# A hybrid decoder layer: six PSUM banks as one tile, loads of the opening moved, memory tokens transposed raw, sample columns kept on chip

## The chip, the cores and the metric

The kernel runs on one core of one Trainium2 chip, in one launch. Its five engines work side by side, each on its own list of instructions: TensorE (PE) multiplies matrices into PSUM, VectorE (DVE) and ScalarE (ACT) do the elementwise work and read PSUM out, GpSimd (POOL) does a little elementwise work in SBUF, and SyncE (SP) issues nearly all DMAs, in order. The metric is the time of the launch on the device in microseconds; the median of several runs is compared, and one further execution is recorded by the hardware profiler.

## The reference

One layer of a decoder for 1024 prompt tokens and 8 sample tokens that share the weights, D = 1024, all in float32:

```
xn = rmsnorm(x)
sc_b, sc_c, sc_x, z, xbc, dt, q, gates = split(xn @ w_in)       # one matrix for all
y_a = (sc_b * conv3(sc_c * sc_x)) @ w_sc_out
xs, B, C = split(silu(conv4(xbc) + bias));  dt = softplus(dt + dt_bias)
y_b = group_rmsnorm((ssd(xs, dt, -exp(a_log), B, C) + d * xs) * silu(z)) @ w_ssm_out
k, v = rmsnorm(mem) @ w_mem_k, rmsnorm(mem) @ w_mem_v           # 256 memory tokens
y_c = softmax(q @ k.T / 16) @ v @ w_attn_o                      # 4 heads x 256
x += (sig(g_a) * y_a + sig(g_b) * y_b + sig(g_c) * y_c) @ w_merge_o
x += (silu(rmsnorm(x) @ w_gate) * (rmsnorm(x) @ w_up)) @ w_down   # 2816 wide
y  = rmsnorm(x)
```

The sample tokens go through the same layer, with cached keys, values, convolution histories and states of their own. The outputs are y for both groups, the memory's keys and values, and the new histories and states.

## The kernel before

**Tiling.** Channels lie on the 128 partitions, tokens along the free axis: 1032 columns, of which the first 1024 are the prompt's and the last 8 the samples'. An operand is kept as two fp32r tiles, a high part (a rounding copy by ScalarE) and a low part (the difference, by VectorE), and a product takes three matmuls: high by high, high by low, low by high. Every weight block and every activation passes through such a split (weights, L162 to L169; split_act, L175 to L179; split_to).

**Two kinds of large product.** gemm (L200) makes one block of 128 output channels for all 1032 columns, in three PSUM banks; L220 is its matmul. strassen (L311) makes two blocks of output channels at once by seven half-size products instead of eight. Each product is st_prod (L260): 24 matmuls, L266, into a pair of banks (516 columns), and each is followed by a read-out, by ScalarE's copy (L321) or VectorE's add or subtract (L319, L380, L395, L398, L408). The weight sums that it needs are made by VectorE (L361, L362, L299, L300) and split (L253 high, L254 low).

**PSUM.** There are eight banks. psm holds two single banks for everything small, taken in turn (sm_ps). The other six are held by one pool at a time. While gemms run, that is pmm: two slots of three banks, taken in turn (mm_ps, L67). While Strassen calls run, it is a pool of three tiles of two banks, with tags m0, m1 and m2 (st_ps). The change from one kind to the other closes one pool and opens the next, four times in all: in front of Z2, behind G18, in front of the feed-forward network and behind d16. A call of strassen takes its first pair (pa), its second (pb) and, where all seven products are needed, its third (pc); calls take the tags forward and backward in turn, apart from the first two calls.

**Order.** The program is written in an order that a list scheduler then makes into one list for each engine: an instruction that is ready early may be moved forward. Three means hold it: in_turn keeps the weight loads and splits in order, issue_after holds an instruction behind another without a wait, and small steps in a queue, pend, are called one by one from within the products by tick(). All loads and most stores are issued by SyncE in list order, and a load whose buffer is not free, or whose source in DRAM is not written yet, holds everything behind it. Staging tiles come from ev, a ring of five; raw weights, high parts and low parts from three rings of three.

**The opening (L461 to L643).** x is loaded in nine token blocks. In three groups of columns (g3 = 0, 1, 2) TensorE transposes x (L549), ScalarE copies the raw transposes out (L530) and SyncE stores them to xT_d (L531); VectorE scales the transposes by the norm (L533), and the result is split (L534, L535). As the groups come, the products of dt (L566, into ps_dt) and of the first B block (L576, into ps_B0) are made. Behind the loop come four blocks of convolution histories: load (L618), eight transposes (L621), copy (L622). Then dt's bias is loaded (L641) and ps_dt is read out with it (L643); two small constants are loaded in the middle of the work of dt (L681, L723). The block C0 follows: its weights, the convolution of B0 (uB, L837; first tap L754 on ScalarE for the prompt's columns, L755 and L758 on VectorE for the samples'), the first half of the Strassen forms (make_raw, L1221 and following, then the splits L416 and L417), C0's gemm, the other half of the forms, z0 (L856) and z1.

**The memory tokens (L1260 to L1325).** Between the products of Z2 and Z4, steps from pend load the 256 tokens, square them (L1274), take the root, scale the tokens by it (L1277), and transpose them in four batches of four (L1284), each batch in one bank. For each of a batch's four transposes ScalarE writes the high part (L1288) and VectorE the low part (L1289), both scaled by the norm's weight and both from PSUM. The K/V products follow in sixteen steps (kv_block), read out by a copy.

**The attention output.** The sample tokens' attention result is transposed into o_s, columns of the tile tri (L1609), and stored to the last eight columns of at_d in DRAM (L1610). Three output products follow one another (out_part); the last takes at_d as operand. out_load (L1400) loads a block of 1032 columns, and the splits L178 and L179 make it an operand. At the end of the kernel down (L1985) adds products of three hidden blocks at a time (pd, read by L2000), behind the last Strassen call d16.

Of the kernel before, what the change touches and what calls it, by code (L numbers as in the profile page):

```python
# [9 lines left out]
F32 = mybir.dt.float32  # L10
# [37 lines left out]
def tile_kernel(ctx: ExitStack, tc, a, o):  # L48
# [14 lines left out]
    psm = ctx.enter_context(tc.tile_pool(name="psm", bufs=2, space=PSUM))  # L63
    mm_stack = ExitStack()
    pmm = [mm_stack.enter_context(tc.tile_pool(name="pmm", bufs=2, space=PSUM))]

    def mm_ps(name):  # L67
        return pmm[0].tile([P, NCH, 512], F32, tag="mm", name=name)

# [163 lines left out]
    HS = [slice(0, HT), slice(HT, TT)]  # L233
    pst = [None]
    freed = [None]
# [21 lines left out]
    def st_ps(tag, name):  # L257
        return pst[0].tile([P, 2, 512], F32, tag=tag, name=name)

# [51 lines left out]
    def strassen(  # L311
# [22 lines left out]
        elif ready is None and early is None:  # L334
            raw1, raw2 = st_raw(src1, f"{nm}r1"), st_raw(src2, f"{nm}r2")
        if count[0] == 0:
            tags = ("m2", "m1", "m0")
        elif count[0] == 1:
            tags = ("m1", "m2", "m0")
        else:  # L340
            tags = ("m0", "m1", "m2") if count[0] % 2 == 0 else ("m2", "m1", "m0")
        count[0] += 1
# [99 lines left out]
    os_d = dram("os_d", [NS, D])  # L442

    tail_sc = cp.tile([P, 1, 10, 8], F32, tag="tail_sc", name="tail_sc")
    tail_xc = cp.tile([P, 3, 11, 8], F32, tag="tail_xc", name="tail_xc")
# [14 lines left out]
    xw = [act_tile(("ah", "al")[k % 2], f"xw{k}", F32) for k in range(KD)]  # L460
    ps_dt, ps_b0 = mm_ps("ps_dt"), mm_ps("ps_B0")  # L461

    with tc.tile_pool(name="p0", bufs=1) as p0:
# [59 lines left out]
        for i in range(3, NCK):  # L523
            load_x(i)
        SY.dma_start(xs_sb, a["x_sample"][:, 0, :])

        def to_xn(k, c, ps, n, name):
# [60 lines left out]
        for g3 in range(3):  # L588
            c, n_all = span(g3)
            for k in range(KD):  # L590
# [12 lines left out]
        while products:  # L603
            products.popleft()()
        for k in range(KD):
            b_product(2, k)
# [3 lines left out]

    for src, dst, nr, nt in (
        (a["state_ssm_conv"][0].rearrange("b j c -> (b j) c"), h_xc, 24, 24),
        (a["state_conv"][0].rearrange("b j c -> (b j) c"), h_sc, 16, 8),
    ):
        per = 8
        for q0 in range(0, nt, per):
            t = ev_tile(f"hist{nr}_{q0}", (nr, per * P))
            SY.dma_start(t, src[:, q0 * P : (q0 + per) * P])  # L618
            ps = sm_ps(f"ps_h{nr}_{q0}")
            for i in range(per):  # L620
                PE.transpose(ps[:, i * nr : (i + 1) * nr], t[:, i * P : (i + 1) * P], ident[:nr, :nr])  # L621
            V.tensor_copy(dst[:, q0 : q0 + per, :].rearrange("p a b -> p (a b)"), ps[:, : per * nr])  # L622
    SY.dma_start(o["s_conv"][0, :, 0, :], a["state_conv"][0, :, 1, :])
# [14 lines left out]
    pd_ = dt_stack.enter_context(tc.tile_pool(name="pdt", bufs=1))  # L638
    bias = pd_.tile([2 * HEADS, 1], F32, tag="bias", name="bias")
    V.memset(bias, 0.0)  # L640
    SY.dma_start(bias[:HEADS], a["ssm_dt_bias"].rearrange("l h -> h l"))  # L641
    dtr = ev_tile("dtr", (2 * HEADS, TT))
    V.tensor_scalar(dtr[:, :TT], flat(ps_dt)[: 2 * HEADS], bias, None, op0=ALU.add)  # L643
    W = 9 * HEADS
# [9 lines left out]
    def dt_softplus():  # L654
# [14 lines left out]
        V.scalar_tensor_tensor(u, x0, -1.0, x0, op0=ALU.mult, op1=ALU.min)  # L669
        S.activation(u, u, AF.Exp)  # L670
        V.tensor_scalar(z, u, 2.0, None, op0=ALU.add)
# [7 lines left out]
        V.scalar_tensor_tensor(dt_flat, q, 2.0, mx, op0=ALU.mult, op1=ALU.add)  # L679
        abc = pd_.tile([P, HEADS], F32, tag="abc", name="abc")  # L680
        SY.dma_start(abc, a["ssm_a_log"][0:1, :].to_broadcast([P, HEADS]))  # L681
        S.activation(abc, abc, AF.Exp)
        V.scalar_tensor_tensor(
# [34 lines left out]
    def dt_sample():  # L718

        esm = pd_.tile([NS, HEADS], F32, tag="esm", name="esm")  # L720
        S.activation(esm, da[:NS, 8, :], AF.Exp)
        exp2 = pd_.tile([16, 2], F32, tag="exp2", name="exp2")
        SY.dma_start(exp2, a["ssm_d"].rearrange("l (t two) -> (l t) two", two=2))  # L723
        ex = pd_.tile([16, 2, 64], F32, tag="ex", name="ex")
# [17 lines left out]
    def proj(col, name):  # L742
        return gemm(weights(wblock(w_in, col), "w" + name), xn, "ps_" + name)

    def conv(acc, u, hist, key, ct, nt, taps, bias):

# [3 lines left out]
        if bias is None:  # L750
            S.activation(acc[:, :T], u[:, 0:T], AF.Copy, scale=w[0])
            V.tensor_scalar(ap_s, hv[:, :, 0], w[0], None, op0=ALU.mult)
        else:
            S.activation(acc[:, :T], u[:, 0:T], AF.Identity, scale=w[0], bias=bias)  # L754
            V.tensor_scalar(ap_s, hv[:, :, 0], w[0], bias, op0=ALU.mult, op1=ALU.add)  # L755
# [470 lines left out]

    def make_forms(k0):
        mk = fx_tile if k0 == 0 else act_pair
        raws = [make_raw(kt) for kt in (k0, k0 + 1)]
        for i, f in enumerate(("T1", "nT2", "T4")):  # L1230
# [39 lines left out]

    def mem_rms():
        for m in range(2):
            junk = memT[m][0].rearrange("p k c -> p (k c)")
            S.activation(junk, mem_sb[m], AF.Square, accum_out=mst[:, m : m + 1])  # L1274
        rsqrt(pm, mrs, mst, D, [P, 2], "m")
        for m in range(2):
            V.tensor_scalar(mem_sb[m], mem_sb[m], mrs[:, m : m + 1], None, op0=ALU.mult)  # L1277

    def mem_t(m, half):
        hi, lo = memT[m]  # L1280
        ps = sm_ps(f"ps_mt{m}{half}")
        for k4 in range(4):
            k = half * 4 + k4
            PE.transpose(ps[:, k4 * P : (k4 + 1) * P], mem_sb[m][:, k * P : (k + 1) * P], ident)  # L1284
        for k4 in range(4):
            k = half * 4 + k4
            pk = ps[:, k4 * P : (k4 + 1) * P]
            S.activation(hi[:, k, :], pk, AF.Copy, scale=par("mem", k))  # L1288
            V.scalar_tensor_tensor(  # L1289
                lo[:, k, :], pk, par("mem", k), f32(hi)[:, k, :], op0=ALU.mult, op1=ALU.subtract  # L1290
            )

    pss_kv = []

    def kv_block(j, q):
# [24 lines left out]
    pend.extend([None, mem_rms, None])  # L1320
    pend.extend(lambda m=m, half=half: mem_t(m, half) for m in range(2) for half in range(2))
    pend.extend(lambda j=j, q=q: kv_block(j, q) for j in range(8) for q in range(2))
    pace[0] = 5
# [6 lines left out]

    mm_stack.close()
    mm_stack = ExitStack()
    st_stack = ExitStack()
    pst[0] = st_stack.enter_context(tc.tile_pool(name="pst1", bufs=1, space=PSUM))
    for i in (2, 4, 6, 8, 10, 12):
# [42 lines left out]
    gate_pair(18, plain)  # L1378
    st_stack.close()
    pa_stack.close()  # L1380
    ch_stack.close()
    pmm[0] = mm_stack.enter_context(tc.tile_pool(name="pmm1", bufs=2, space=PSUM))

# [14 lines left out]
    def out_load(src, k):  # L1398
        t = ev_tile(f"in0{k}")
        SY.dma_start(t[:, :TT], src[k])  # L1400
        ahead.append(t)
# [98 lines left out]
    if True:  # L1500
# [3 lines left out]
        vl = at.tile([P, 2, D], F32R, tag="vl", bufs=1, name="vl")  # L1504
        o_s = tri[:, :64].rearrange("p (t b) -> p t b", t=8)
        sc_s = tri[:, 64:].rearrange("p (m b h) -> p m b h", m=2, b=NS)
# [96 lines left out]
        def s_back():  # L1603
# [5 lines left out]
            V.tensor_copy(o_s.rearrange("p t b -> p (t b)"), ps[:, :64])  # L1609
            SY.dma_start(at_d[:, :, T:TT].rearrange("t p b -> p t b"), o_s)  # L1610

# [209 lines left out]
    aux_stack.close()  # L1821
    mm_stack.close()

# [3 lines left out]
    st_stack = ExitStack()  # L1827
    pst[0] = st_stack.enter_context(tc.tile_pool(name="pst", bufs=1, space=PSUM))
    pfx = st_stack.enter_context(tc.tile_pool(name="fx", bufs=2))
# [135 lines left out]
    st_stack.close()  # L1965
    pmm[0] = ctx.enter_context(tc.tile_pool(name="pmm2", bufs=2, space=PSUM))
    fin = ctx.enter_context(tc.tile_pool(name="fin", bufs=1))
# [131 lines left out]
```

## Time and profile before

| | |
|---|---|
| median of 3 runs | 2475.04 us (2474.16 to 2475.89) |
| the profiled execution | 2474.8 us, span 2472.7 us |
| granted TensorE clock, mean | 0.994 |
| TensorE busy | 2428.5 us (98%) |
| VectorE, ScalarE, GpSimd busy | 1584.3, 1067.1, 114.8 us |
| opening up to the first C0 matmul | 58.73 us |
| C0, z0, z1 up to the first Strassen matmul | 58.73 to 98.74 us |
| DMA | 404.42 MB, mean 164 GB/s |

A page of the profile gives for each engine the time in which it executes, and for each group of instructions how long its engine stood idle before it and which instruction ended that (the releaser). In a timeline a row is: start in us, duration in us, engine, line, operation, output <- input, shape, count, and in brackets the idle time before and the releaser. A row with a count gives several instructions in one. The table of stretches gives, for each, its length, the busy time of each engine with the number of its instructions, the granted TensorE clock (1.00 is full speed), the share of the DMA engines and GB/s.

### The profile page before, as it was taken

What the parts mean: (1) busy time and instruction counts of PE and PEld (TensorE: products, weight loads), DVE (VectorE), ACT (ScalarE), POOL (GpSimd) and SP (SyncE); (2) the same over time, 40 slices, a digit from 0 to 9 for tenths busy, and PEclk for the clock granted to TensorE, in tenths of its full rate; (3) what the DMA queues carried; (4) which work ended last, traced back from release to release, by engine and by line L of the source; (5) the groups of instructions that cost most, each with busy time, mean ns of one, the idle gap of its engine ahead of it and who ended that gap; (6) DMA issues with size and microseconds to landing.
All of it is one profiled execution on the core that took longest, in us unless ns stands there. A gap on an engine that the chain in (4) does not pass through costs nothing.

```text
span 2472.7 us, 45688 instructions
## 1 busy us (share of the span) xinstructions
PE 2428.5 (98%) x18946; PEld 2310.5 (93%) x18946; DVE 1584.3 (64%) x2601; ACT 1067.1 (43%) x1712; POOL 114.8 (5%) x163
## 2 busy tenths in 40 slices
PE   8999999999999999999999999999999999999998
PEld 6899999999999999888888888899999999999998
DVE  6844586777677774666767562454787555476755
ACT  6654455354545535556545441223453333342322
POOL 0100000000000000121120000000000000000000
PEclk8999999999999999999999999999999999999999
DMA  6344434344344456667878677874454323264421
GB/s 195 121 139 154 132 102 153 112 130 131 108 137 137 129 154 210 194 207 254 265 219 286 205 265 238 266 241 153 141 174 134 108 86 112 74 231 132 156 85 69
DMA packets 359662, 404.42 MB, mean 164 GB/s; under 512 B 17446, under 2 KB 286870, under 8 KB 359447
## 3 DMA queue, kind: packets, MB, share of 16 engines
q1 hardware_dynamic: 339006, 343.79, 44.6%
q10 hardware_dynamic: 20449, 57.71, 6.0%
q8 instruction: 149, 2.44, 0.4%
q14 instruction: 58, 0.48, 0.1%
HBM read 286.35 MB, written 115.32 MB: 162 GB/s over the span
## 4 chain that ended last, share of the span: by engine, by line
PE 86%; DMA 5%; DVE 5%; ACT 2%; issue 1%; SPq 0%; ACTq 0%; POOL 0%; DVEq 0%
PE po L220 12%; PE ps_q L220 4%; PE pm L1800 3%; PE ps_g L220 2%; PE pd L220 1%; PE py L1041 1%; PE pss L1054 1%; PE po L1033 1%; PE Z2m L266 1%; PE Z4m L266 1%; PE X8m L266 1%; PE d12m L266 1%; PE C2m L266 1%; PE C4m L266 1%; PE G18m L266 1%
## 5 line engine op out<-in xcount | busy, mean ns | idle before, releaser
L986 ACT ACTIVATE r<-r,acum 128x128 f32<-128x128 f32 x256 | 79.2, 392 | 5.1 <-DMA r<-ac_d 4.7
L757 DVE SCALAR_TENSOR_TENSOR ax<-u,prm,ax 128x1024 f32<-128x1024 f32 x44 | 56.3, 1279 | 0.0
L927 ACT ACTIVATE st<-st,es 128x128 f32<-128x128 f32 x128 | 41.5, 392 | 26.4 <-DMA st<-in_state_ssm_dram 23.9
L1018 POOL TENSOR_TENSOR xdd<-xdt,decst 128x512 f32<-128x512 f32 x32 | 37.1, 1160 | 292.2 <-DVE xdt L1014 292.2
L1447 DVE TENSOR_TENSOR yr<-po,yr 128x1032 f32<-128x1032 f32 x8 | 9.8, 1230 | 55.1 <-PE po L220 45.2
L1037 DVE TENSOR_TENSOR y<-po,ea 128x512 f32<-128x512 f32 x28 | 19.3, 690 | 38.9 <-PE po L1033 38.9
L1012 DVE TENSOR_TENSOR r<-r,cbm 128x1024 f32<-128x1024 f32 x32 | 39.2, 1224 | 2.5
L929 DVE SCALAR_TENSOR_TENSOR st<-sr,dts,st 128x128 f32<-128x128 f32 x128 | 40.3, 345 | 0.4
L1011 ACT COPY bT<-bp 128x128 f32<-128x128 f32 x32 | 8.5, 265 | 64.3 <-DVE cbm L1009 64.2
L2034 ACT ACTIVATE fj<-psy 128x512 f32<-128x512 f32 (+1 forms) x18 | 10.7, 596 | 59.1 <-PE psy L2032 59.0
L933 DVE SCALAR_TENSOR_TENSOR sr<-st,sr 128x128 f32<-128x128 f32 x128 | 35.2, 285 | 1.1
L1054 PE MATMUL pss<-xdd,bT 128*128 128x512 f32 x64 | 33.4, 604 | 2.3 <-ACT bT L1011 2.3
L1041 PE MATMUL py<-r,xdt 128*64 128x128 f32 x512 | 35.0, 279 | 0.0
L987 ACT ACTIVATE r<-r 128x1024 f32<-128x1024 f32 x32 | 33.9, 1058 | 0.7
L1014 DVE TENSOR_TENSOR xdt<-xp,dtT 128x512 f32<-128x512 f32 x32 | 21.9, 684 | 18.7 <-PE xp L1007 18.5
L1807 DVE TENSOR_TENSOR x<-pm,xT 128x516 f32<-128x516 f32 x16 | 11.1, 695 | 35.1 <-PE pm L1800 35.1
L1067 POOL TENSOR_TENSOR s<-s,cdec 128x512 f32<-128x512 f32 x28 | 32.1, 1145 | 4.5 <-DVE s L1060 3.9
L1041 PEld LDWEIGHTS py<-r,xdt 128*64 128x64 f32 x512 | 27.3, 136 | 4.2 <-issue 0.5
L1033 PE MATMUL po<-bc,s 128*128 128x128 f32 x224 | 29.6, 275 | 0.0
L760 DVE SCALAR_TENSOR_TENSOR ax<-u,prm,ax 128x1032 f32<-128x1032 f32 x22 | 28.3, 1286 | 0.0
L1178 DVE SCALAR_TENSOR_TENSOR x<-x,prm,sqa 128x1032 f32<-128x1032 f32 x16 | 19.7, 1288 | 13.3 <-ACT sqa L1174 13.3
L1033 PEld LDWEIGHTS po<-bc,s 128*128 128x128 f32 x224 | 27.7, 191 | 0.5
(9066 smaller groups left out, 9044.0 us busy)
## 6 DMA issues: line engine op xcount, KB each, us to landing
r<-ac_d SPq DMA_DIRECT2D x32, 512.0 KB
gt<-gt_d SPq DMA_DIRECT2D x24, 516.0 KB
xs_d<-ax ACTq DMA_DIRECT2D x22, 516.0 KB
gt_d<-G ACTq DMA_DIRECT2D x20, 516.0 KB
x<-xs_d SPq DMA_DIRECT2D x16, 516.0 KB
zs<-zs_d SPq DMA_DIRECT2D x16, 516.0 KB
yb_d<-x SPq DMA_DIRECT2D x16, 516.0 KB
in<-yb_d SPq DMA_DIRECT2D x16, 516.0 KB
```

The source lines that it names most:

```text
L220: PE.matmul(out[:, c : c + n], wt[:, ks], x[:, c : c + n], start=(k == 0 and i == 0), stop=(k == nk - 1 and i == 2),)
L266: PE.matmul(hv(ps)[:, c : c + n], wt[:, ks], x[:, c : c + n], start=(start and kt == 0 and i == 0), stop=(kt == 3 and i == 2), skip_group_ ...
L757: V.scalar_tensor_tensor(acc[:, :T], u[:, j : j + T], w[j], acc[:, :T], op0=ALU.mult, op1=ALU.add)
L927: S.activation(st[:, i], st[:, i], AF.Copy, scale=es[:, g * 4 + i, b : b + 1])
L929: V.scalar_tensor_tensor(st[:, i], rb, dts[:, g * 4 + i, b : b + 1], st[:, i], op0=ALU.mult, op1=ALU.add)
L986: S.activation(r[:, j, :], r[:, j, :], AF.Relu, scale=-1.0, bias=acum[:, c, h : h + 1])
L1012: V.tensor_tensor(r, r, bc(cbm.unsqueeze(1), [P, HPG, P]), op=ALU.mult)
L1018: G.tensor_tensor(b3(xdd, HPG), b3(xdt, HPG), bc(decst[:, c, hs].unsqueeze(2), [P, HPG, 64]), op=ALU.mult)
L1033: PE.matmul(po[:, t * P : (t + 1) * P], state["s"][:, t * P : (t + 1) * P], bcg[1][:, cs], start=True, stop=True,)
L1041: PE.matmul(py[hp : hp + 64, (h // 2) * P : (h // 2 + 1) * P], xdt[:, h * 64 : (h + 1) * 64], r[:, (h % 2) * 4 + h // 2, :], start=True, s ...
L1054: PE.matmul(pss, bT, xdd, start=True, stop=True)
L1800: PE.matmul(hv(ps)[:, c : c + n], wt[:, ks], x[:, half * HT + c : half * HT + c + n], start=(k == 0 and i == 0), stop=(k == KD - 1 and i = ...
```

## The change

Four parts, in one:

- **Six banks as one tile.** pmm and the Strassen pools go; one tile, six, of six banks lives through the whole kernel. mm_ps gives its lower or its upper three banks in turn (side); st_ps gives the pair of banks 0-1, 2-3 or 4-5 by the tag. The tags now go forward and backward in turn from the first call on, and each call sets the side that the next gemm will take. In the opening ps_B0 has the lower side and ps_dt the upper one, and C0 takes the upper.
- **The opening.** The bias and the two constants are loaded right behind x, into a pool that stays. The raw weights of C0 are loaded at the beginning of group 1; those of z0 and z1 and the four history blocks at the beginning of group 2. ps_dt is read out as soon as the dt products are done, ahead of the last group of B0's products, and C0's weights are split right behind that. The forms, C0 and z0 are held behind the last history copy (past) and the first tap of B0's convolution (tap). Of the four make_raw only two stand ahead of that mark. The Exp of the decay is held behind the Exp of dt.
- **The memory tokens** are transposed as loaded. VectorE multiplies a whole batch by the norm's weight out of PSUM, back into the tile of the tokens; ScalarE copies the high part and VectorE subtracts, both from SBUF. The root comes behind the transposes, and K and V are scaled by it when they are read out.
- **The sample columns.** The store to at_d's last eight columns goes; out_load takes 1024 columns from at_d and copies the other eight from o_s, with GpSimd.

```diff
+    six = pbig.tile([P, 2 * NCH, 512], F32, tag="six", name="six")
+    side = [0]
     def mm_ps(name):
-        return pmm[0].tile([P, NCH, 512], F32, tag="mm", name=name)
+        i = side[0]
+        side[0] = 1 - i
+        return six[:, NCH * i : NCH * (i + 1)]
...
     def st_ps(tag, name):
-        return pst[0].tile([P, 2, 512], F32, tag=tag, name=name)
+        i = int(tag[1:])
+        return six[:, 2 * i : 2 * i + 2]
...
+        tags = ("m0", "m1", "m2") if count[0] % 2 == 0 else ("m2", "m1", "m0")
+        side[0] = 1 - count[0] % 2
...
+            if g3 == 1:
+                loaded["wC0"] = load_raw(wblock(w_in, C_XBC + 20 * P), "wC0")
+            if g3 == 2:
+                for i in range(2):
+                    loaded[f"wz{i}"] = load_raw(wblock(w_in, C_Z + i * P), f"wz{i}")
+                for src, dst, nr, nt in past_of:
...
+        dtr = ev_tile("dtr", (2 * HEADS, TT))
+        turned = V.tensor_scalar(dtr[:, :TT], flat(ps_dt)[: 2 * HEADS], bias, None, op0=ALU.add).ins
+        with tc.issue_after(turned), tc.issue_after(ins):
+            w_c0 = weights(None, "wC0")
         for k in range(KD):
             b_product(2, k)
...
-    w_c0 = weights(wblock(w_in, C_XBC + 20 * P), "wC0")
     xbc_tile(16, "B0", ps_b0)
-    make_forms(0)
-    xbc_tile(20, "C0", w=w_c0)
-    make_forms(2)
-    z_step(0)
+    raws = [make_raw(kt) for kt in (0, 1)]
+    with tc.issue_after(past), tc.issue_after(tap[0]):
+        make_forms(0, raws)
+        xbc_tile(20, "C0", w=w_c0)
+        make_forms(2)
+        z_step(0)
...
-        for k4 in range(4):
-            k = half * 4 + k4
-            pk = ps[:, k4 * P : (k4 + 1) * P]
-            S.activation(hi[:, k, :], pk, AF.Copy, scale=par("mem", k))
-            V.scalar_tensor_tensor(
-                lo[:, k, :], pk, par("mem", k), f32(hi)[:, k, :], op0=ALU.mult, op1=ALU.subtract
-            )
+        ks = slice(half * 4, half * 4 + 4)
+        w = prm[:, PC["mem"] + half * 4 : PC["mem"] + half * 4 + 4]
+        t = b3(mem_sb[m][:, half * 512 : half * 512 + 512], 4)
+        V.tensor_tensor(t, b3(ps, 4), bc(w.unsqueeze(2), [P, 4, P]), op=ALU.mult)
+        S.copy(hi[:, ks], t)
+        V.tensor_sub(lo[:, ks], t, f32(hi[:, ks]))
...
-            S.copy(t[:, m, :], pss_kv[m][:, :256])
+            S.activation(t[:, m, :], pss_kv[m][:, :256], AF.Copy, scale=mrs[:, m : m + 1])
...
+        if src is at_d:
+            SY.dma_start(t[:, :T], src[k, :, :T])
+            G.tensor_copy(t[:, T:TT], o_s[:, k, :])
...
-            SY.dma_start(at_d[:, :, T:TT].rearrange("t p b -> p t b"), o_s)
```

More of the change, by code (lines that the diff above doesn't have):

```diff
@@ L589, in tile_kernel @@
             c, n_all = span(g3)
+            if g3 == 1:
[4 more added lines that the diff above has]
+                for src, dst, nr, nt in past_of:
+                    for q0 in range(0, nt, 8):
+                        t = ev_tile(f"hist{nr}_{q0}", (nr, 8 * P))
+                        SY.dma_start(t, src[:, q0 * P : (q0 + 8) * P])
+                        hists.append((t, dst, nr, q0))
             for k in range(KD):
@@ L608, in tile_kernel @@
         SY.dma_start(r_d, rbc[0:1, :])
[L611 to L622, printed above, removed]
+    for t, dst, nr, q0 in hists:
+        ps = sm_ps(f"ps_h{nr}_{q0}")
+        for i in range(8):
+            PE.transpose(ps[:, i * nr : (i + 1) * nr], t[:, i * P : (i + 1) * P], ident[:nr, :nr])
+        past = V.tensor_copy(dst[:, q0 : q0 + 8, :].rearrange("p a b -> p (a b)"), ps[:, : 8 * nr]).ins
     SY.dma_start(o["s_conv"][0, :, 0, :], a["state_conv"][0, :, 1, :])
@@ L1274, in mem_rms, with mem_root @@
             S.activation(junk, mem_sb[m], AF.Square, accum_out=mst[:, m : m + 1])
+    def mem_root():
         rsqrt(pm, mrs, mst, D, [P, 2], "m")
-        for m in range(2):
-            V.tensor_scalar(mem_sb[m], mem_sb[m], mrs[:, m : m + 1], None, op0=ALU.mult)
     def mem_t(m, half):
```

65 lines of the change are left out of this document (28 added, 37 removed).

## The prediction

> **What bounds the kernel now.** I read the page first, then the waits of TensorE in order of size, then a table of stretches around each wait, then the timelines of those stretches.
>
> ```profile
> span 2472.7 us, 45688 instructions
> PE 2428.5 (98%) x18946; PEld 2310.5 (93%) x18946; DVE 1584.3 (64%) x2601; ACT 1067.1 (43%) x1712; POOL 114.8 (5%) x163
> ```
> ```profile
> PE ps_C L220 <- ACT uB L837: 4.2, 1, 4.2
> PE psp L1647 <- ACT pr L1553: 3.5, 1, 3.5
> ...
> PE ps_mt L1284 <- DVE meml L1289: 2.1, 1, 2.1
> ```
> TensorE works 2428.5 of 2472.7 us, and the change takes no matmul away. So at most the 44.2 us in which TensorE stands still can go, with what a lowered clock costs behind them. The largest single wait is the one that ends the opening, and the third largest here is in the memory tokens; the second (scores against probabilities, psp) is not touched.
>
> ```profile
> 54.50:58.70 4.20, 0.00 (x0) 0.00 (x0) 4.07 (x8) 3.02 (x4) 0.00 (x0) 0.63 0.56 122
> 58.70:63.40 4.70, 4.67 (x18) 4.11 (x18) 4.70 (x10) 3.61 (x5) 1.27 (x2) 0.60 1.09 295
> ...
> 54.90:98.30 43.40, 38.41 (x237) 34.34 (x237) 42.78 (x76) 30.18 (x39) 10.35 (x5) 0.92 0.46 141
> ```
> The columns are stretch, length, busy time of PE, PEld, DVE, ACT and POOL, granted clock, DMA share and GB/s. TensorE does nothing for 4.20 us, and then runs 4.70 us at a granted clock of 0.60. Over the whole stretch to 98.30 it is VectorE that is full: 42.78 of 43.40 us.
>
> **The opening and the first Strassen pair.** C0 stands still for a bank, for its weights, or for both:
>
> ```profile
> 52.20 2.28 PE L621 MATMUL ps_h<-ident,hist 24*128 24x24 f32 x32
> 58.73 1.20 PE L220 MATMUL ps_C<-xnh,wC0h 128*128 128x512 f32 x3 [4.25 <-ACT uB L837]
> ```
> ```profile
> 52.91 0.85 DVE L622 COPY h_xc<-ps_h 128x192 f32<-128x192 f32 x2 [1.76 <-PE ps_h L621]
> ...
> 56.17 1.22 DVE L169 TENSOR_TENSOR wC0l<-wC0r,wC0h 128x1024 fp32r<-128x1024 f32 x1
> 57.31 1.28 DVE L643 TENSOR_SCALAR dtr<-ps_dt,bias 64x1032 f32<-64x1032 f32 x1
> ```
> ```profile
> 50.47 0.42 SPq L140 DMA_DIRECT2D wC0r<-in_w_in_dram  x1
> ```
> The wait is put down to the copy of B0, but the two accumulators are taken in turn, and C0's is the one of ps_dt, which is read out at 57.31 to 58.59, just before 58.73. Ahead of that stands the split of C0's weights (56.17), whose load SyncE issued only at 50.47. The change moves both: the load and the bias go in front of the transposes of the last groups, the read-out of ps_dt right behind the last dt product, and the split behind it. The 1.28 and 1.22 us then fall into VectorE's 1.76 us of idle time ahead of 52.91 and the gaps around the history copies. C0 can start at 54.48, where the history transposes end: 4.25 us, and with no pause nothing lowers the clock: 4.67 us at 0.60 hold 4.67 x 0.40 = 1.87 us of lost work.
>
> The second wait is where the pools used to change, at the first Strassen pair Z2:
>
> ```profile
> 98.74 0.50 PE L266 MATMUL Z2m<-xnh,Z2Ah 128*128 128x256 f32 x2 [1.60 <-ACT z L858]
> ...
> 101.70 0.40 PE L266 MATMUL Z2m<-T10ah,Z2Sh 128*128 128x256 f32 x2
> ```
> ```profile
> 99.66 1.22 DVE L254 TENSOR_TENSOR Z2Sl<-Z2sa,Z2Sh 128x1024 fp32r<-128x1024 f32 x1 [1.40 <-ACT Z2Sh L253]
> ```
> Z2's first product waited 1.60 us for z1 to be read out. Now it takes the two banks that z1 does not use, and its second product, 2.96 us later, the ones that z1 used. TensorE alone would thus gain 4.25 + 1.87 + 1.60 = 7.7 us. But the product T1 needs Z2Sl, which VectorE finishes at 100.88, and VectorE has no slack: it can come forward only by the idle time it loses, 0.62 us (43.40 - 42.78), and by the work that it can do ahead of 54.90, at most some 2.0 us (1.76 and the 0.27 between the copies). Then Z2Sl is there at 98.3, T1 starts about 0.5 us before it (the first two pairs of matmuls do without it): 97.8 against 101.70, a gain of 3.9. I take 4.5, near the VectorE bound, since the list order is made anew and the new order keeps the forms' work behind the history and the first conv tap; the ends are 1.9 (the wait comes back in front of T1 and lowers the clock as it does now, 3.9 - 1.87 with rounding) and 7.7.
>
> What is moved forward is some ten loads (wC0, two z blocks, four history blocks, the bias, two constants). Each holds SyncE's queue some 0.42 us, as wC0r's row does, so 4 us spread over the opening; behind them stand the stores of the raw transposes, which free only a ring of five staging tiles. I cost it at nothing, at most 0.5 us if a tile of that ring is late. The Exp of the decay, ordered behind another Exp, spares ScalarE a table change; ScalarE has 13 of 43 us free in that stretch, so it is worth nothing.
>
> **The memory tokens.**
>
> ```profile
> 120.29 1.42 DVE L1277 TENSOR_SCALAR mem<-mem,mrs 128x1024 f32<-128x1024 f32 x2
> 122.25 0.35 DVE L1289 SCALAR_TENSOR_TENSOR meml<-ps_mt,prm,memh 128x128 fp32r<-128x128 f32 x1 [0.55 <-ACT memh L1288]
> ```
> ```profile
> 125.38 0.66 PE L1284 MATMUL ps_mt<-ident,mem 128*128 128x128 f32 x4 [2.12 <-DVE meml L1289]
> ...
> 127.38 0.58 PE L266 MATMUL Z4m<-T10ah,Z4Sh 128*128 128x256 f32 x1 [0.47 <-ACT Z4Sh L253]
> ```
> ```profile
> 127.38:129.40 2.02, 2.02 (x9) 2.02 (x10) 1.66 (x4) 2.00 (x8) 0.00 (x0) 0.50 0.00 0
> 129.40:133.00 3.60, 3.60 (x27) 3.60 (x26) 2.43 (x7) 3.00 (x12) 0.00 (x0) 0.82 0.00 0
> ```
> Each batch of four transposes holds its bank while ScalarE and VectorE take turns on it four times, and the whole stands behind the root and the scaling at 120.29. So the third batch waits 2.12 us, the work behind it 0.47, and then 2.02 x 0.50 + 3.60 x 0.18 = 1.66 us go to the clock: 4.25 us in all. After the change the transposes need no root, and the bank is free after one multiplication of 128x512, which I price at 0.69 us by the Strassen row of 128x516 below; copy and subtraction follow from SBUF. VectorE's sum does not grow: four batches of two 0.69 us passes are 5.5 us, against sixteen of up to 0.35 and the 1.42. The root moves behind the transposes and is needed first by the K/V read-out, which now scales by it in the ScalarE pass that copied before. I take 3.5; ends 2.5 (a bank still waits) and 4.2.
>
> Here a rule can be weighed. The clock fell after a pause of 2.12 us, to 0.50. The Trainium skill (TensorE: Matmul & The Clock Gate, "What's actually happening") says that the clock halves after an idle window of about 3.4 us, free-running; by it this stage would lose no clock, and the gain here would be 2.6 us. The trace does not agree with it for a pause this short, and the sum goes by the trace.
>
> **The sample columns of the attention output.**
>
> ```profile
> 1572.61 0.43 SPq L1610 DMA_DIRECT2D at_d<-tri  x1
> ...
> 1577.03 2.98 SPq L1400 DMA_DIRECT2D in<-at_d  x3
> ```
> ```profile
> 1582.48 0.74 PE L220 MATMUL po<-b00h,wo30h 128*128 128x512 f32 x3 [0.87 <-ACT b00h L178]
> 1583.74 0.73 PE L220 MATMUL po<-b00l,wo30h 128*128 128x512 f32 x3 [0.53 <-DVE b00l L179]
> ```
> The loads of the next operand stood behind the store of eight columns. Without the store they need not wait on it, and the eight columns come by a small copy on GpSimd, off the loads' own columns:
>
> ```profile
> 971.97 0.33 POOL L807 COPY qs<-q 128x8 f32<-128x8 f32 x1 [12.02 <-ACT q L806]
> ```
> That copy, 0.33 us, lies beside the load. The two waits are 1.40 us; I take 1.1, ends 0.3 and 1.4, as SyncE's own queue may still be what is late.
>
> **The seam after the last Strassen call.**
>
> ```profile
> 2377.60 0.69 DVE L408 TENSOR_TENSOR x<-x,d16m 128x516 f32<-128x516 f32 x1 [1.26 <-PE d16m L266]
> ```
> ```profile
> 2378.44 0.71 PE L220 MATMUL pd<-h16h,wd160h 128*128 128x512 f32 x3 [0.87 <-DVE x L408]
> ```
> pd waited for a pool to close. In one tile, the side is chosen so that pd has the three banks away from d16's last pair: 0.9 gained, ends 0.6 and 0.9. At the two other seams TensorE waits for no bank now, so nothing is to be had.
>
> **Sum.** 4.5 + 3.5 + 1.1 + 0.9 = 10.0 us. The profiled execution took 2474.8 us (span 2472.7 and 2.1 around it), 0.24 below the median of the three, 2475.04; from the median: 2465.0. The low ends add up to 5.3 and the high ones to 14.2; with 3 us either way for waits that a new list order shifts (psp's 3.5 us alone is such a wait), the likeliest case's own range is 2457 to 2473.
>
> **The rivals.**
>
> *One tile, one lock (slower).* All large products now write into one tile of six banks. Is a write into one bank held until a read of another bank is over? One place in the profile speaks for it, a tile of three banks at the end of the kernel:
>
> ```profile
> 2415.87 0.34 PE L2060 MATMUL pl<-h21h,wl0l 128*128 128x384 f32 x1
> ...
> 2416.92 0.34 PE L2060 MATMUL pl<-h21h,wl1l 128*128 128x384 f32 x1
> ```
> ```profile
> 2417.29 1.49 DVE L2062 TENSOR_TENSOR x<-pl,x 128x384 f32<-128x384 f32 x3 [3.46 <-PE pl L2060]
> ```
> The first bank is finished by the row of 2415.87, at 2416.21, yet its read starts at 2417.29, behind the last matmul into the third bank. Against it stands a tile in SBUF, of which two engines write different columns at one time:
>
> ```profile
> 60.11 0.21 DVE L758 SCALAR_TENSOR_TENSOR aB<-h_xc,prm,aB 128x8 f32<-128x8 f32 x1
> ```
> ```profile
> 60.12 1.23 ACT L754 ACTIVATE aB<-uB,prm 128x1024 f32<-128x1024 f32 x1
> ```
> Price: each product is followed by a read, and the next product would wait for it as pd waits now, 0.87 us. The matmuls of all calls:
>
> ```profile
> 0.00:2472.70 2472.70, 1410.32 (x11760) 1402.48 (x11760) 0.99 0.51 164
> 0.00:2472.70 2472.70, 622.46 (x3600) 527.11 (x3600) 0.99 0.51 164
> ```
> (L266, then L220.) 11760 / 24 = 490 products, 426 us; and of the three-bank tiles some 83 (about 55 at L220, 16 in the merge, 12 at the end), by the width twice as long, about 1.4 us each, 117 us. In all 2475 + 543 - 10 = 3008 us. It decides from the first call on, and turns on this alone: whether a write after a read is held across banks. pl's row is a read after writes, which a signal given only at the end of a group of matmuls would explain as well, and a write waits for VectorE's or ScalarE's signal, given by every read. I give it 0.18. The Trainium skill (PSUM — Partial Sum Buffer, "Summary: rules for kernel authors") has a read beside running matmuls aim at a different bank, and asks for a guard by bank only; by it the chip needs no such wait and the time would be 2465, and whether the program waits all the same, no run here shows.
>
> *VectorE becomes the bound of the opening.* Speaking for it: 42.78 of 43.40 us busy. The wait moves from C0 to T1 and lowers the clock there; the opening gives 1.9, with memory 2.5, the at_d loads 0.6 and the seam 0.9 that is 5.9: 2469 us. Chance 0.14.
>
> *Nothing that can be measured.* The stalls go, and the new order puts others of their size elsewhere (a psp wait of 3.5 us twice, a load late behind the moved ones): gain 2, 2473 us. Chance 0.12. That the change does not do what it says would look the same.
>
> **How the numbers follow.** Forecast 0.56, VectorE 0.14, nothing 0.12, one lock 0.18. A measurement of this kernel can tell 0.2% from no change, 5.0 us, so faster means below 2470.1. Faster: 0.55 of the forecast, 0.10 of VectorE, 0.01 of nothing, 0.66. Same: 0.01 + 0.04 + 0.09, 0.14. Slower: 0.18 + 0.02, 0.20. The range 2457 to 2477 leaves out the lock (0.18) and little else; it reaches past the forecast's own 2473 for the case of nothing.
>
> **What would show it.** Right: ps_C's first matmul near 54.5 with no wait and a clock near 1.00 behind it; no wait of Z2's first product on z, a wait of up to 4 us before T1 if VectorE binds; ps_mt without a wait of 2 us and clock 1.00 from 127 to 133; no at_d store, its loads issued before 1577 less the gain so far; pd without its 0.87. Wrong: waits of 0.6 to 0.9 us ahead of hundreds of products, with TensorE's share at 80% of the span, is the lock; a 4 us wait with a clock of 0.6 ahead of T1 is VectorE; new waits at psp, pss or pskT by as much as was gained are the third case.

## The result and the profile after

The changed kernel takes 3163.19 us (median of 4 runs, 3156.4 to 3166.64) against 2475.47 us before: a ratio of 1.2773, 95% interval 1.2750 to 1.2797. All medians here are of fast executions; two slow ones, of the columns alone (8977.5 us) and of the opening without the hold (3144.7 us at a granted clock of 0.70), are left out. The profiled execution took 3156.4 us, its span is 3154.7 us. The page of the changed kernel begins:

```profile
span 3154.7 us, 45650 instructions
PE 2600.1 (82%) x18946; PEld 2373.3 (75%) x18946; DVE 1604.2 (51%) x2591; ACT 1073.5 (34%) x1701; POOL 123.2 (4%) x171
```

The same 18946 matmuls, and VectorE and ScalarE work about as long as before (1604.2 and 1073.5 us against 1584.3 and 1067.1). TensorE now stands idle for 554.6 us instead of 44.2, and it is busy for 171.6 us more with the same work: 510.4 and 171.6 make up the 682.0 us by which the span has grown. Its waits, the largest groups first, with the sum, the count and the longest:

```profile
PE six L269 <- ACT u L324: 27.5, 33, 1.5
PE six L269 <- ACT G L324: 27.1, 30, 1.5
PE six L269 <- DVE x L322: 22.9, 23, 1.9
...
PE six L223 <- DVE gt L1741: 11.4, 7, 3.1
...
PE six L223 <- DVE x L2009: 9.6, 7, 1.4
```

There is no one long wait; there are hundreds of short ones, nearly all of a product (L269, L223: the lines L266 and L220 of before) for a read-out of the product ahead of it. One product of the changed kernel, TensorE's timeline and then ScalarE's:

```profile
502.78 0.50 PE L269 MATMUL six<-T10ah,C0Sh 128*128 128x256 f32 x2 [0.68 <-ACT c L324]
503.12 0.40 PE L269 MATMUL six<-T10al,C0Sh 128*128 128x256 f32 x2
...
505.49 0.39 PE L269 MATMUL six<-T12ah,C0Sl 128*128 128x256 f32 x2
506.57 0.50 PE L269 MATMUL six<-nT20ah,C0Sh 128*128 128x256 f32 x2 [0.68 <-ACT su L324]
```
```profile
505.92 0.59 ACT L324 COPY su<-six 128x516 f32<-128x516 f32 x1 [2.89 <-PE six L269]
```

By the program, the product that starts at 506.57 goes into another pair of banks (pa) than the one that ScalarE reads from 505.92 to 506.51 (pb), and still it starts only behind that read. In the kernel before, where the pairs were tiles of their own, the two run side by side (TensorE, then ScalarE):

```profile
101.70 0.40 PE L266 MATMUL Z2m<-T10ah,Z2Sh 128*128 128x256 f32 x2
101.94 0.40 PE L266 MATMUL Z2m<-T10al,Z2Sh 128*128 128x256 f32 x2
```
```profile
101.90 0.59 ACT L321 COPY Z<-Z2m 128x516 f32<-128x516 f32 x1 [2.27 <-PE Z2m L266]
```

So this is the rival that the prediction called one tile, one lock. The theory to be tested: a write into any bank of a tile waits for the reads of the whole tile that stand ahead of it in the program. The rivals: the new order of sides and tags puts products on banks that are really being read; or one of the other three parts is slow by itself.

### The profile page after: what moved, and what is told of

The parts are those of the page before. It is cut to its first block, busy times and chain, and to the rows that moved or that the text cites. A ratio compares the mean times of both kernels' runs of the same rounds, so it can differ in the third digit from the quotient of the medians.

```text
span 3154.7 us, 45650 instructions
## 1 busy us (share of the span) xinstructions
PE 2600.1 (82%) x18946; PEld 2373.3 (75%) x18946; DVE 1604.2 (51%) x2591; ACT 1073.5 (34%) x1701; POOL 123.2 (4%) x171
## 5 line engine op out<-in xcount | busy, mean ns | idle before, releaser
L322 DVE TENSOR_TENSOR x<-six,x 128x516 f32<-128x516 f32 x24 | 16.6, 694 | 44.1 <-PE six L269 44.1
L1819 DVE TENSOR_TENSOR x<-six,xT 128x516 f32<-128x516 f32 x16 | 11.1, 695 | 50.5 <-PE six L1812 48.2
L324 ACT COPY u<-six 128x516 f32<-128x516 f32 x33 | 19.4, 587 | 48.5 <-PE six L269 42.5
L1461 DVE TENSOR_TENSOR yr<-six,yr 128x1032 f32<-128x1032 f32 x8 | 9.8, 1230 | 47.4 <-PE six L223 47.4
L1741 DVE TENSOR_TENSOR gt<-six,gt 128x1032 f32<-128x1032 f32 x8 | 9.9, 1232 | 44.3 <-PE six L223 44.3
L2071 DVE TENSOR_TENSOR x<-six,x 128x384 f32<-128x384 f32 (+2 forms) x32 | 11.9, 420 | 35.9 <-PE six L2069 35.8
```

## The experiments

Each was timed in turn with the kernel before, on the same chip; the groups ran on different chips, so a time is compared with the one of the kernel before in its own row, and the difference in us is between these two medians.

| kernel | us | before | ratio, 95% interval |
|---|---|---|---|
| the change | 3163.2 | 2475.5 | 1.2773 (1.2750 to 1.2797) |
| three parts, separate pools | 2487.9 | 2477.3 | 1.0041 (1.0028 to 1.0053) |
| the tile alone | 3158.9 | 2477.3 | 1.2749 (1.2730 to 1.2769) |
| pairs in one tile | 3032.5 | 2477.3 | 1.2245 (1.2228 to 1.2261) |
| gemm sides in one tile | 2606.2 | 2477.3 | 1.0519 (1.0505 to 1.0534) |
| the change, six tiles of one bank | 2487.0 | 2475.5 | 1.0048 (1.0035 to 1.0061) |
| memory alone | 2468.9 | 2476.2 | 0.9970 (0.9958 to 0.9982) |
| columns alone | 2473.7 | 2476.2 | 0.9992 (0.9984 to 1.0001) |
| opening alone | 2487.4 | 2476.2 | 1.0045 (1.0032 to 1.0058) |
| opening, no hold | 2493.2 | 2475.8 | 1.0070 (1.0051 to 1.0089) |
| opening, early splits | 2477.7 | 2476.2 | 1.0008 (0.9999 to 1.0016) |
| memory and columns | 2468.0 | 2475.5 | 0.9973 (0.9963 to 0.9983) |
| three parts, early splits | 2468.4 | 2475.5 | 0.9973 (0.9962 to 0.9984) |
| the change, six tiles, early splits | 2468.8 | 2475.5 | 0.9977 (0.9967 to 0.9988) |
| three parts, early splits, no hold | 2465.9 | 2475.8 | 0.9961 (0.9948 to 0.9974) |

### Is it the tile?

**The three other parts, with the pools of before.** The edit takes six, side and the new tags out of the changed kernel and puts the pools back.

> The changed kernel with the separate PSUM pools of before; the opening, the memory tokens and the sample columns stay changed. Theory (one lock: a write into one bank of a tile waits for the read of another bank of the same tile): the whole slowdown goes, and what is left is the forecast's sum without the two seams, 10.0 - 1.6 - 0.9 = 7.5 us, 2468 us. Rival (one of the other three parts is slow by itself): still far above 2475, over 2600 us.

2487.9 us: the slowdown of 688 us goes, so the tile holds it. But the three parts are slower by 10.6 us instead of faster by 7.5; that is taken up below.

**The tile alone**, in the kernel before.

> The kernel before with the one tile of six banks, its tags and sides, and nothing else changed. Theory (one lock): about 2475 + 690 = 3170 us, since 490 half-size products and some 83 three-bank tiles each wait for the read before. Rival (other parts): 2475 us. Rival (the new tags and sides put a product on banks that are just being read): also slow; the next two runs part it from the theory.

3158.9 us, 681.6 more than before.

**The pairs in one tile**, and nothing else moved:

```diff
     def st_ps(tag, name):
-        return pst[0].tile([P, 2, 512], F32, tag=tag, name=name)
+        i = int(tag[1:])
+        return pst[1][:, 2 * i : 2 * i + 2]
...
     pst[0] = st_stack.enter_context(tc.tile_pool(name="pst1", bufs=1, space=PSUM))
+    pst[1] = pst[0].tile([P, 6, 512], F32, tag="six", name="six")
```

> The kernel before, in which only the three bank pairs of the Strassen calls become slices of one tile; every product keeps the banks, the order and the pool changes that it had. Theory (one lock): 490 products at 0.95 us (a product's pitch of 3.79 us in the changed kernel against 2.84) or more where the read is longer: 2940 to 3090 us. Rival (new tags and sides): 2475 us, since no bank changes.

3032.5 us, 555.1 more: 1.13 us for each of 490 products. Every product keeps the pair of its tag and its place in the order, so new tags and sides are not needed for the slowdown. The page:

```profile
span 3029.4 us, 45648 instructions
PE 2554.9 (84%) x18946; PEld 2343.8 (77%) x18946; DVE 1601.2 (53%) x2601; ACT 1071.6 (35%) x1712; POOL 115.8 (4%) x163
```

Against the kernel before TensorE is idle for 430.3 us more (474.5 against 44.2), 0.88 us a product, and busy for 126.4 us more, 0.26 us a product.

**The gemm sides in one tile**, in the same way:

```diff
-        return pmm[0].tile([P, NCH, 512], F32, tag="mm", name=name)
+        if pmm[0] is not mine[0]:
+            mine[:] = [pmm[0], pmm[0].tile([P, 2 * NCH, 512], F32, tag="mm", name="six"), 0]
+        i = mine[2]
+        mine[2] = 1 - i
+        return mine[1][:, NCH * i : NCH * (i + 1)]
```

> The kernel before, in which only the two three-bank slots of the gemms become halves of one tile, banks and order kept. Theory (one lock): some 83 tiles at 1.2 to 1.6 us, 2575 to 2610 us, and this rise and the one of the pairs add up to the rise of the tile alone. Rival (new tags and sides): 2475 us.

2606.2 us, 128.9 more: 1.55 us for each of some 83 tiles. The two rises add up to 684.0; the tile alone cost 681.6. The page:

```profile
span 2603.8 us, 45685 instructions
PE 2474.5 (95%) x18946; PEld 2340.1 (90%) x18946; DVE 1588.1 (61%) x2601; ACT 1069.3 (41%) x1714; POOL 118.4 (5%) x163
```

Here TensorE is idle for 85.1 us more and busy for 46.0 us more. The mean granted clock is 0.981, against 0.994 in the kernel before and 0.993 with the pairs, so that part of the 46.0 us is a lowered clock.

**Six tiles of one bank**, in the changed kernel: the banks, sides and tags of the change, and no pool that closes. A read-out that spans banks becomes one instruction for each bank.

```diff
-    six = pbig.tile([P, 2 * NCH, 512], F32, tag="six", name="six")
+    six = [pbig.tile([P, 512], F32, tag=f"six{i}", name=f"six{i}") for i in range(2 * NCH)]
...
     def flat(ps):
-        return banks(ps)[:, Z0 : Z0 + TT]
+        return Multi([(ps[0][:, Z0:512], 0, 256), (ps[1], 256, 512), (ps[2][:, : TT - 768], 768, TT - 768)])
```

> The changed kernel whole, but the tile of six banks is six tiles of one bank each: same banks, same sides and tags, no pool that closes; a read-out is cut at the bank limits into two or three instructions. Theory (the wait goes by the tile, not by the choice of banks): the 690 us go, and what remains is the three parts and the seams: 2480 to 2490 us, with the starved split of z0 still in it, less about 2.5 us for the seams. Rival (the new sides and tags themselves collide): over 2600 us.

2487.0 us. The page of that kernel:

```profile
span 2486.1 us, 46290 instructions
PE 2429.3 (98%) x18946; PEld 2310.8 (93%) x18946; DVE 1606.5 (65%) x2941; ACT 1086.6 (44%) x1973; POOL 129.7 (5%) x171
```

TensorE is back at 98%, with the very banks of the change, though VectorE and ScalarE have 622 instructions more. The wait goes by the tile, not by the bank: the matmuls and the banks they go to are those of the change, so it is the program that waits and not the chip. That each read-out is cut by bank here is not the reason either: in the kernel before, one read-out of two banks ran beside matmuls into another pair (101.90, above).

The place at the end of the kernel from which the prediction argued, three banks and one read-out of each, shows the same thing in small. With six tiles of one bank its rows are (TensorE, the last matmul into the first bank and into the third, then VectorE; L91 is the helper through which read-outs go here):

```profile
2429.76 0.34 PE L2107 MATMUL six<-h21h,wl0l 128*128 128x384 f32 x1
...
2430.80 0.34 PE L2107 MATMUL six<-h21h,wl1l 128*128 128x384 f32 x1
```
```profile
2430.13 1.60 DVE L91 TENSOR_TENSOR x<-six,x 128x384 f32<-128x384 f32 x3 [2.54 <-PE six L2107]
```

The first bank is finished at 2430.10 and its read starts at 2430.13, 1.01 us before the last matmul into the third bank ends. In the kernel before, with one tile for the three, it started behind that matmul. The matmuls are grouped as before, so a signal that comes only at the end of a group is not the reason.

The two waits at the seams are gone from this profile (Z2 on z, pd on d16's read-out), but the 2.5 us do not show in the time: against the kernel before in its own row it is 11.5 us slower, the three parts with pools 10.6, which the runs cannot tell apart.

### Why do the three parts lose?

**Each part alone.**

> The kernel before with the memory part alone (raw transposes, one multiplication per batch, the root behind, K and V scaled at the read-out). My sum: 3.5 us faster, 2.5 to 4.2; the wait of 2.12 us at ps_mt and the clock of 0.50 behind it go. Rival: the waits only move (to the K/V read-out, which now needs the root): within 1 us of before.

2468.9 us, 7.3 faster. The stretches of the kernel before, then of this one:

```profile
120.00:130.00 10.00, 7.26 (x47) 6.44 (x46) 7.18 (x17) 9.34 (x24) 0.00 (x0) 0.86 0.26 107
130.00:140.00 10.00, 10.00 (x81) 9.83 (x81) 4.08 (x9) 4.96 (x14) 0.00 (x0) 0.96 0.18 56
```
```profile
120.00:130.00 10.00, 10.00 (x87) 10.00 (x87) 7.85 (x15) 8.00 (x12) 0.00 (x0) 1.00 0.26 107
130.00:140.00 10.00, 10.00 (x87) 10.00 (x86) 3.08 (x4) 7.57 (x19) 0.00 (x0) 1.00 0.49 159
```

The pause is gone and the clock stays at 1.00, as the step said.

> The kernel before with the sample columns alone (no store to at_d, eight copies on GpSimd). My sum: 1.1 us faster, 0.3 to 1.4. Rival: the loads wait for SyncE's own queue as before: no change.

2473.7 us: 2.5 us below before, but the interval reaches 1.0001. In the profile SyncE issues the first two loads at 1573.05, and in place of four waits there, 1.8 us in all, is one of 0.5 us:

```profile
1573.05 1.72 SPq L1402 DMA_DIRECT2D in<-at_d  x2
```
```profile
PE po L220 <- ACT b05h L178: 0.5, 1, 0.5
```

> The kernel before with the opening alone, separate pools. With all three parts the split of z0's low weights stood 33 us behind its high part on VectorE and TensorE idled 19.1 us. Theory (the opening part alone starves that split): about 15 us slower, 2490 us, with a wait of 17 to 21 us between C0 and z0. Rival (it takes the memory part's or the columns' steps as well): no such wait, 2470 to 2474 us.

2487.4 us, 11.2 slower: it is the opening. What happens shows best in the run of the three parts. Its stretches:

```profile
60.00:70.00 10.00, 9.83 (x64) 8.64 (x61) 10.00 (x23) 4.92 (x8) 3.77 (x2) 1.00 0.14 54
70.00:80.00 10.00, 1.16 (x6) 0.86 (x6) 8.37 (x11) 7.22 (x9) 1.00 (x2) 0.76 0.00 0
80.00:90.00 10.00, 0.00 (x0) 0.00 (x0) 10.00 (x22) 3.67 (x5) 10.00 (x1) 0.50 0.13 53
90.00:100.00 10.00, 9.69 (x46) 8.50 (x47) 5.89 (x10) 2.09 (x5) 1.40 (x1) 0.71 0.78 219
```

TensorE stops for 19 us in the middle of z0 (the first two busy times are those of TensorE and its weight loads), while VectorE is nearly full. TensorE, then ScalarE and VectorE on z0's weights:

```profile
54.92 1.23 PE L220 MATMUL ps_C<-xnh,wC0h 128*128 128x512 f32 x3 [0.39 <-ACT uB L852]
...
90.31 1.19 PE L705 MATMUL ps_ac<-da,tri 128*128 128x256 f32 x2 [19.15 <-issue]
```
```profile
57.14 1.04 ACT L168 CAST wz0h<-wz0r 128x1024 fp32r<-128x1024 f32 x1
```
```profile
72.01 1.28 DVE L772 SCALAR_TENSOR_TENSOR aC<-uC,prm,aC 128x1024 f32<-128x1024 f32 x1 [1.63 <-ACT aC L769]
...
90.13 1.21 DVE L169 TENSOR_TENSOR wz0l<-wz0r,wz0h 128x1024 fp32r<-128x1024 f32 x1
```

C0 starts at 54.92, where the prediction put it. The high part of z0's weights is ready at 58.18, the low part at 91.34, 33 us later. In the kernel before, VectorE made that split right behind the read-out of ps_dt:

```profile
58.70 1.21 DVE L169 TENSOR_TENSOR wz0l<-wz0r,wz0h 128x1024 fp32r<-128x1024 f32 x1
```

My reading is that the late read-out of ps_dt and the late copy of B0 had left nothing else that was ready just then. With those out of the way the scheduler always finds VectorE something ready that stands earlier in the program, and the split, written behind all the forms, comes last in the list. It is a matter of the list and not of the moment: at 70.38 VectorE stands idle for 1.63 us with the split's input long there.

**The opening without the hold** on past and tap, which could also keep the split back:

```diff
-    raws = [make_raw(kt) for kt in (0, 1)]
-    with tc.issue_after(past), tc.issue_after(tap[0]):
-        make_forms(0, raws)
...
+    make_forms(0)
```

> The opening alone without the hold: the forms, C0 and z0 are not kept behind the last history copy and the first tap; all four differences of the forms may go forward as before. Theory (the split of z0 is last because it is last in the program and VectorE, no longer waiting for C0, has ready work without a gap): still a wait of 17 to 20 us ahead of z0, 2484 to 2490 us. Rival (the hold keeps the split back): the wait goes, 2470 to 2476 us.

2493.2 us, 17.4 slower and above the 2484 to 2490 that were expected. The hold is not it: the stop is still there, and here the profile names the split as what ends it:

```profile
90.40 0.80 PE L220 MATMUL ps_z<-xnh,wz0l 128*128 128x512 f32 x1 [18.83 <-DVE wz0l L169]
```

**The opening with early splits.** The splits of z0 and z1 are written behind the first half of the forms:

```diff
         make_forms(0, raws)
+        w_z += [weights(None, f"wz{i}") for i in range(2)]
         xbc_tile(20, "C0", w=w_c0)
```

> The opening alone, with one more edit: the splits of z0's and z1's weights are written ahead of C0's convolution and of the second half of the forms, so that they come earlier in the lists. Theory (TensorE idles because VectorE, which is full, takes the splits last of all, as they are last in the program): the 19 us go, and the opening gives what VectorE lets it, 2 to 5 us faster than before, 2470 to 2473 us. Rival (VectorE's whole work sets the end of the stretch, whatever its order): the wait moves behind z0 or z1, about as slow as the opening alone.

2477.7 us, the same as before within 0.2%. The 19 us are gone, and Z2 starts 8.5 us earlier than before. But X17, 175 us on, starts 1.5 us later than before. Between the two its waits are

```profile
PE Z4m L266 <- ACT Z4Ah L253: 3.2, 1, 3.2
PE ps_mt L1302 <- DVE mem L1295: 2.3, 1, 2.3
```

Theory and rival were both half right: the order caused the stall, and what it then gains is spent a little later.

**Put together.**

> The memory part and the columns together, the opening and the pools as before. If they add up: 7.3 + 2.0, 2467 us. If the list made anew moves other waits by as much: within 3 us of that either way.

2468.0 us. That is within the 3 us of a sum, and no more than memory alone gave: 7.5 us against 7.3.

> The opening, the memory tokens and the sample columns, separate pools, with the splits of z0 and z1 written early. Alone, the opening so ordered starts Z2 8.5 us earlier than before and loses it again around the memory tokens' transposes. Theory (what took it back is the old memory stage: waits at ps_mt and Z4 and the clock behind them): with the raw transposes it stays, 2455 to 2463 us. Rival (VectorE, now ahead of TensorE by nothing, makes it wait at the next place): 2466 to 2469 us, no better than memory and columns.

2468.4 us: the rival. Z2 starts 7.5 us earlier than before, Z6 7.1, X17 5.4; with memory alone Z6 is 5.8 and X17 5.6 earlier. So the opening, even with its order mended, adds nothing that lasts. Of the lead at Z2, 1.2 us are only work put off: eight transposes of the work on dt (ps_acT) now stand behind Z2's start instead of ahead of it.

> The same with the early splits of z0 and z1. Theory: the three parts with the early splits, less 2.5 us for the seams at Z2 and at d16, plus what the cut read-outs cost VectorE in the opening, where it is full (some 0.2 us for each of a handful): within 3 us of the run of the three parts with early splits. Rival (the cut read-outs, about 570 of them, show all along): 10 us or more above it.

2468.8 us, within the expected 3 us of the three parts with early splits.

> The three parts with the early splits, and without the hold. If the hold costs or gives something once the splits are early, it shows against the run with the hold (2468.4 us): theory (VectorE is full either way, only its order moves): within 4 us of it.

2465.9 us, the lowest of all; its interval (0.9948 to 0.9974) overlaps that of the three parts with the hold (0.9962 to 0.9984), so whether the hold costs anything here is not settled. It is 0.39% below the kernel before.

## Why the prediction was wrong

**The step that failed is the weighing of the lock.** The prediction gave it 0.18, and left it out of the range. It had the one row that decides, pl's read that waited for the last matmul into another bank of its tile, and explained it away: "which a signal given only at the end of a group of matmuls would explain as well". The runs show that the row meant what it said: with tiles of one bank the same read starts with its own bank (2430.13). The row that it set against it, two engines writing different columns of one tile side by side, was of a tile in SBUF; PSUM tiles are not treated so here. The rule of the Trainium skill that was quoted (PSUM — Partial Sum Buffer, "Summary: rules for kernel authors": aim at a different bank) agrees with the runs as far as the chip goes: in the kernel before and with six tiles of one bank, matmuls and read-outs of different banks run together. The program waits all the same when the banks are slices of one tile, and that was said to be open.

**The lock's price was too small.** Put at 543 us, measured at 681.6. The place and the count were right: 490 products, and the rises of pairs and sides add up. A product costs 1.13 us instead of 0.87, a three-bank tile 1.55 instead of 1.4. The idle time was priced nearly right, 426 and 117 us against 430.3 and 85.1 measured; what was left out is that TensorE also gets busier. Idle time leaves out what a stop costs it in overlap: in the product shown, the first pair of matmuls is followed after 0.34 us instead of 0.24, and the last pair has to end (0.39 instead of 0.24), so 0.68 of idle time is 0.93 us of time. These 0.25 us are what the run of the pairs shows, 0.26 a product. With the gemm sides the clock comes on top.

**The opening** was to gain 4.5 us (1.9 to 7.7; by its own sum the low end is 2.0, and 1.6 of the high end needed the new banks), and alone it loses 11.2. The forecast of C0's start (54.5; measured 54.92) and of VectorE as the next bound held, but the hand-over to z0 was taken to follow by itself. What it missed is that the list is made by what is ready: a split that was early because VectorE stood idle becomes late when VectorE does not. It had asked what is late next, and looked at T1, 40 us on, instead of at the operand of the next gemm, z0. With the splits written early the gain at Z2 is 8.5 us, above the forecast, and it does not last.

**The memory tokens** were to gain 3.5 us (2.5 to 4.2) and gain 7.3. The mechanism was right. At Z6, behind the stage, the gain is 5.8 us, against the 4.25 of waits and clock that the prediction counted; the rest comes later, among other places at psp, whose wait went from 3.5 to 2.0 us, which the remade list brought and nothing in the step. What the 1.5 us beyond the counted waits are was not taken apart; stops that break the overlap, as above, would be one reason.

**The sample columns**, 1.1 us (0.3 to 1.4): 2.5 measured, not to be told from nothing; the waits went as forecast. **The seams**, 2.5 us: with six tiles of one bank the waits go, but the time gains -0.9 and -0.4 us, in two pairs of runs, against a noise of some 3 us: not seen.

Where the opening's 8.5 us go can be counted between the starts of Z2 and X17. There the opening with early splits takes 184.4 us, the kernel before 174.4. TensorE is idle for 7.0 us instead of 2.7; the granted clock takes about 5 us instead of about 2 (0.93 over the 70.1 us to Z6, against 0.97 over 61.7); the transposes of ps_acT are 1.2; and the 384 matmuls of the K/V products follow one another more slowly. The first and the last of a block of 24, with memory alone and with the opening alone:

```profile
120.88 0.28 PE L1307 MATMUL ps_kv<-wkv00h,memh 128*128 128x256 f32 x1
...
123.51 0.28 PE L1309 MATMUL ps_kv<-wkv00l,memh 128*128 128x256 f32 x1
```
```profile
137.01 0.28 PE L1323 MATMUL ps_kv<-wkv00h,memh 128*128 128x256 f32 x1
...
139.75 0.28 PE L1325 MATMUL ps_kv<-wkv00l,memh 128*128 128x256 f32 x1
```

That is 0.114 and 0.119 us from one to the next, at a clock of 1.00, and so in the other undisturbed blocks: 0.114 in the kernel before, with memory or the columns, 0.119 in every run with the opening. Over 384 matmuls it is some 2 us. Together these are about the 10 us. With the memory tokens mended, the same counts make up most of what the opening loses there against memory alone (176.5 against 168.8 us). Why the K/V matmuls are slower with the opening stays open.

## What to carry to other kernels

Before several PSUM banks become slices of one tile, look in a profile for a read of one bank that waits for a write of another bank in the same tile: if there is one, every hand-over between matmuls and read-outs will wait, and banks that are to work side by side must be tiles of their own. Where a list scheduler orders the work, a stall that is removed takes away the gap in which something else got done early: ask which operand of the next step was made in that gap, and write it earlier in the program. And a stop of TensorE costs more than the idle time in front of the first matmul: here 1.13 us a product, of which 0.88 is idle time.

## What the runs showed of the hardware

The prediction took it that with no pause nothing lowers the clock. It can fall although TensorE is not idle. In the run of the three parts with early splits it is busy without a gap from 105 to 120 us:

```profile
110.00:113.00 3.00, 3.00 (x32) 2.54 (x31) 1.67 (x3) 0.00 (x0) 0.00 (x0) 1.00 0.01 3
113.00:117.00 4.00, 4.00 (x26) 3.97 (x25) 2.24 (x7) 2.70 (x5) 0.00 (x0) 0.61 0.02 4
117.00:120.00 3.00, 3.00 (x25) 2.84 (x24) 2.38 (x6) 2.91 (x5) 0.00 (x0) 0.96 0.00 0
```

4 us at 0.61 are about 1.6 us lost. Just ahead of it lie three batches of eight small transposes each (8 by 8), begun within 2.6 us, between the products:

```profile
110.15 0.66 PE L746 MATMUL ps_ex<-ident,exs 8*128 8x8 f32 x8
111.41 0.66 PE L746 MATMUL ps_ex<-ident,exs 8*128 8x8 f32 x8
112.67 0.66 PE L746 MATMUL ps_ex<-ident,exs 8*128 8x8 f32 x8
```

That these count as little work for the clock is not shown, and the early splits are not the reason either. With memory alone the three batches start at 111.02, 112.16 and 113.43, and the clock stays at 1.00; with memory and columns, where TensorE does the same in the same order up to there, they start at 110.94, 112.09 and 113.36, and it falls:

```profile
114.00:117.70 3.70, 3.70 (x20) 3.69 (x19) 2.38 (x6) 3.30 (x7) 0.00 (x0) 0.54 0.32 94
```

With six tiles and early splits it stays at 1.00 from 100 to 120 us. So one and the same stretch loses this time in one execution and not in another. What decides it was not found; a difference of 1.7 us between two single profiles can be this and nothing else.
